# Seven products for two more pairs in the third group of both feed-forward stages, and another order at the head of the kernel

## The chip, the cores and the metric

The kernel runs on one core of one Trainium2 chip. The metric is the device time of one execution in microseconds (us); the time of a kernel is the median of its runs. Matmuls run on TensorE (PE, with its weight loads shown as PEld), elementwise work on VectorE (DVE) and ScalarE (ACT), and transfers are issued by SyncE (SP), by ACT's queue and by GpSimd (POOL).

## The reference

One layer of a hybrid encoder block over 256 tokens of width 2048, all in float32. The change concerns the two feed-forward stages (FFN 1 at the start, FFN 2 at the end) and the norm in front of FFN 1:

```python
x = x + 0.5 * swiglu(rms_norm(x, ffn1_norm[l]), ffn1_w_up[l], ffn1_w_down[l])
h = rms_norm(x, mix_norm[l])
proj = h @ w_in[l]
...                                   # two recurrent branches, gates, cross attention
x = x + 0.5 * swiglu(rms_norm(x, ffn2_norm[l]), ffn2_w_up[l], ffn2_w_down[l])
return rms_norm(x, final_norm)
```

with `swiglu(h) = (silu(gate) * up) @ w_down`, where `gate` and `up` are the halves of `h @ w_up`. The inner width is 5632.

## The kernel before, in words

**Precision.** Each float32 operand is split into a high part, rounded to the type `float32r` that PE multiplies, and a low part, the rest. A product is then three matmuls: high by high, low by high, high by low (`three`, L446). The high part is rounded by ACT (`split`, L120), the low part is the difference, taken by DVE (L121).

**Feed-forward order.** The 5632 inner columns fall into 11 groups (g = 0 to 10) of 512. For each group there are 8 *pairs* (p = 0 to 7), each 256 of the 2048 rows of the up weights, held in one weight tile of 128 x 2048 elements. Behind a group come *downs*: one tile of the down weights each, for an earlier group, 24 matmuls. Group 0 is followed by none, groups 1 and 2 by two downs each, groups 3 to 10 by four. `ffn_order` (L42) writes this order out, once for both stages; `PRODUCTS` (L458) says what each kind of pair multiplies:

- *plain* (group 0): 8 products, 24 matmuls.
- *fast*: a pair of 2 x 2 blocks by Strassen-like sums, 7 products, 21 matmuls. Its weights need sums of the blocks (`td`, three DVE subtractions, L213 to L215), and high and low parts of both the blocks and the sums: on ACT one rounding of 128 x 1536 and two of 128 x 1024, on DVE one difference of 128 x 1536 (`l`) and two of 128 x 1024 (`tl`).
- *mixed*: 8 products whose results fit the accumulators of a fast group; 24 matmuls, weights split as a plain tile.

Groups 1 and 2 alternate mixed and fast (four of each). From group 3 on p = 0 and p = 6 are mixed and the other six fast, in the order p = 1, 3, 0, 4, 2, 6, 5, 7.

**How a weight tile is prepared.** `weights` (L165) works through the plan of all tiles two ahead of their use. `prepare` (L195) has SP load the tile into one of three `raw` buffers (L71, taken in turn) and splits it into `h` and `l` (three buffers each). From group 3 on a mixed tile is *added* (L133): `begin_added` (L186), called one tile earlier, loads `raw`, has ACT write its rounded negative into `l` (L191) and has POOL issue a transfer that adds `raw` to that (`accum_op`, L192), which leaves the low part in `l`; `prepare` then only rounds `raw` into `h` (L200). No DVE work is in it, and 32 such transfers are in the kernel.

**Behind a group.** The eight accumulators are combined by DVE and ACT (`ends`, L529 to L532, when the last pair that uses accumulator 0 is through; `last`, L533 to L543), put through `activate` (L478), turned by PE transposes and split again (`turn`, L483, `hidop`).

**The head.** 16 matmuls on a tile of ones (`warm`, L109) run before the first data are there. ACT's queue loads the norm weights and small parameters (`vt`, 168 columns, L99). `head_x(p)` (L572) has SP load 512 columns of x for a pair, then `operand_pairs` (L406) scales them by the norm's weights on ACT into `xg` (two instructions of 128 x 256, L412) and splits `xg` into `xh` and `xl`. The first four weight tiles come in four cuts each. `rest` (L162) holds work put behind a given tile of the plan, such as the sums of x's blocks (L432) that fast and mixed pairs need. The first eight tiles are issued in program order on SP, ACT and DVE (L170, L179); after that the order is the scheduler's. `parameters` (L611), a chain of small ACT and DVE steps on `vt` for the recurrent branches, is called from `to_mix` (L642) and held behind the last residual update so far by `issue_after`.

Of the kernel before, what the change touches and what calls it, by code (L numbers as in the profile page):

```python
# [8 lines left out]
F32 = mybir.dt.float32  # L9
F32R = mybir.dt.float32r  # L10
ACT = mybir.ActivationFunctionType
ALU = mybir.AluOpType

P = 128
T = 256
# [12 lines left out]
VEC = {}  # L28
# [13 lines left out]
def ffn_order():  # L42

    out, down = [("plain", 0, p) for p in range(8)], [("down", 0, 1, c, 0) for c in range(4)]
    for g in range(1, NG):
        if g < 3:  # L50
            out += [(("mixed", "fast")[p % 2], g, p) for p in (0, 1, 2, 3, 5, 4, 7, 6)]
        else:
            out += [("mixed" if p in (0, 6) else "fast", g, p) for p in (1, 3, 0, 4, 2, 6, 5, 7)]
        if g > 2 and g % 2:
            down = [("down", g - 2, 2, c, b) for c in range(4) for b in (g - 2, g - 1)]
        n = 2 if g < 3 else 4
        out, down = out + down[:n], down[n:]
    return out + [("down", NG - 2, 2, c, b) for c in range(4) for b in (NG - 2, NG - 1)]
# [3 lines left out]
def block_kernel(ctx: ExitStack, tc: tile.TileContext, xT, xin, memT, vec, gfin, bgate, lruw, wu1, wd1, win, wv,  # L62
                 wg, wab, wout, wq, wk, wvm, wo, wu2, wd2, out_):
    nc = tc.nc
    pe, dve, act, sp = nc.tensor, nc.vector, nc.scalar, nc.sync
# [21 lines left out]
    def slot(dt=F32, name="slot"):  # L87
        return slots.tile([P, 1024], dt, name=name, tag="slot")
# [4 lines left out]
    def bank(name="acc"):  # L93
        return psum.tile([P, 512], F32, name=name, tag="acc")


    vt = const.tile([P, NVEC], F32, name="vt")
    small_n = VEC["ident"][0]
    act.dma_start(vt[:, :small_n], vec[:, :small_n])  # L99

    def col(name, i=0, n=1):
        a = VEC[name][0] + i
        return vt[:, a:a + n]
# [1 line left out]
    ones = const.tile([P, P], F32, name="ones")  # L105
    dve.memset(ones, 1.0)
    warm = bank("warm")
    for _ in range(16):
        pe.matmul(warm[:, :P], ones, ones, start=True, stop=True)  # L109
    eps = const.tile([P, 1], F32, name="eps")  # L110
    act.activation(eps, ones[:, :1], ACT.Copy, scale=EPS)
# [4 lines left out]
    done = {}  # L116


    def split(h, l, raw):
        done["high"] = act.activation(h, raw, ACT.Copy).ins  # L120
        done["low"] = dve.tensor_tensor(out=l, in0=raw, in1=h.bitcast(F32), op=ALU.subtract).ins  # L121
# [4 lines left out]

    plan, ahead = [], []
    orders = dict.fromkeys(("ffn1", "ffn2"), ffn_order())

    def plan_ffn(name, wu, wd):  # L130
        for e in orders[name]:
            src = wd[e[4], e[3]] if e[0] == "down" else wu[e[1], e[2]]
            kind = "fast" if e[0] == "fast" else "added" if e[0] == "mixed" and e[1] > 2 else "plain"  # L133
            plan.append(((name,) + e, src, kind))

    def plan_columns(name, w, which):
# [2 lines left out]
    def plan_rows(name, w, g):  # L139
        plan.extend(((name, g, kq), w[g, kq], "plain") for kq in range(w.shape[1]))  # L140

    plan_ffn("ffn1", wu1, wd1)
    for hf in range(2):
        for base in (8, 0):
# [11 lines left out]
    for name, w in (("mv", wvm), ("o", wo)):  # L156
        for g in range(4):
            plan_rows(name, w, g)
    plan_ffn("ffn2", wu2, wd2)

    head, rest = [], {}
# [204 lines left out]
    def root_ready(x):  # L366

        root = small.tile([P, 1], F32, name="root", tag="root")
        act.activation(root, x[:, :1], ACT.Abs)
        act.activation(root, root, ACT.Sqrt)  # L370
# [21 lines left out]
    def normed(ops, c, gain):  # L392

        accs = turned(xt[c])
        for m in range(4):
            ops.add(accs[m // 2][:, m % 2 * T:][:, :T], col(gain, 4 * c + m))
# [6 lines left out]
    BOTH = [2, 4]  # L403
    xd = []

    def operand_pairs(src, gain, q, xg, out):  # L406

        for a in src:
            i = len(out)
            g = xg[:, i * 512:(i + 1) * 512]  # L410
            for z in range(2):
                act.activation(g[:, z * T:][:, :T], a[:, z * T:(z + 1) * T], ACT.Copy,  # L412
                               scale=col(gain, 4 * q + 2 * i + z))
            h, l = slot(F32R, "xh"), slot(F32R, "xl")
            split(h[:, :512], l[:, :512], g)
            less = None if i else (h[:, 512:768], l[:, 512:768])
            if 2 * q + i in BOTH:
                if 2 * q + i == BOTH[0]:
                    xd.append(slot(F32R, "xd"))
                n = 512 * BOTH.index(2 * q + i)  # L420
                less = [xd[-1][:, a:a + 256] for a in (n, n + 256)]
            out.append(((h, l), less))

        def sums(which=((0, "less"), (0, "sums"), (1, "less"), (1, "sums"))):
            s = slot(name="xs")
            for i, ((h, l), less) in enumerate(out):
                a = [xg[:, i * 512 + j * P:][:, :P] for j in range(4)]

                def made(h, l, n, at, terms):
                    o = [s[:, at + j * P:][:, :P] for j in range(n)]  # L430
                    for j, (x, y, op) in enumerate(terms(o)):
                        dve.tensor_tensor(out=o[j], in0=x, in1=y, op=op)  # L432
                    split(h, l, s[:, at:at + n * P])

                if less and (i, "less") in which:
                    made(*less, 2, 0, lambda o: ((a[0], a[1], ALU.subtract), (a[2], a[3], ALU.subtract)))
                if (i or 2 * q in BOTH) and (i, "sums") in which:
                    if not i and len(which) > 1:
                        s = slot(name="xs")
                    made(h[:, 512:], l[:, 512:], 4, 512 * i,  # L440
                         lambda o: ((a[1], a[3], ALU.add), (o[0], a[0], ALU.subtract),
                                    (a[1], a[0], ALU.subtract), (a[2], o[1], ALU.subtract)))

        return sums
# [127 lines left out]
    def head_x(p):  # L572

        q = p // 2
        if p % 2 == 0:
            xq[q] = slot(name="xf"), slot(name="xg"), []
        src, xg, out = xq[q]
        a = p % 2 * 512
        sp.dma_start(src[:, a:a + 512], xT[:, p * 512:(p + 1) * 512])
        sums = operand_pairs([src[:, a:a + 512]], "ffn1_norm", q, xg, out)  # L580
        if p % 2:
            sums1.append(sums)
        pairs1.append(out[-1])

    def head_residual(i):
# [4 lines left out]
        if i:  # L590
            sp.dma_start(vt[:, small_n:NVEC], vec[:, small_n:])

    head += [lambda p=p: head_x(p) for p in range(8)]
    for i in range(2):
        rest[4 + i] = lambda i=i: head_residual(i)
# [46 lines left out]
    def to_mix(c, t):  # L642
        sq2.add(c, [t])
        if t == 0:
            return
        if c == 0:
            with tc.issue_after(done["residual"]):
                parameters()
        if c == 2:
            root_ready(xt[c])  # L650
        if c < 3:
            normed(xs2, c, "mix_norm")
        else:
            late2.append(lambda: normed(xs2, c, "mix_norm"))

    with scope(**FFN_POOLS):
        ffn("ffn1", pairs1, sq1, to_mix)
# [393 lines left out]
    def to_ffn(c):  # L1051
        out = []
        sums2.append(operand_pairs(turned(xt[c]), "ffn2_norm", c, slot(name="xg"), out))
        pairs2.extend(out)
        if c < 2:
            sums2.pop(0)()
# [130 lines left out]
```

## Time and profile before

| | |
|---|---|
| median of 3 runs | 2441.59 us (2441.09 to 2441.65) |
| the profiled execution's own time | 2441.09 us |
| its span | 2439.3 us |
| granted TensorE clock | 0.999 |
| PE busy | 2428.9 us (100% of the span), 12250 matmuls |
| DVE busy | 1889.8 us (77%) |
| ACT busy | 1394.5 us (57%) |
| DMA | 509.69 MB, 209 GB/s on average |
| accumulating transfers by POOL | 32 |

The profile shows one execution. The span is the stretch from the first to the last record; the execution's own time has 1.8 us more around it. A row of the timeline gives start, duration, engine, line, operation and `out<-in` tiles with their shape; `xN` is the number of like instructions put in one row, and brackets give the engine's idle time before the row with what ended it. A row of a table of stretches gives the stretch, its length, then busy time and number of instructions of PE, PE's weight loads, DVE, ACT and POOL, then clock, DMA share and GB/s. A row of waits names the waiting instruction, what it waited for, total us, times and longest. Matmuls are pipelined: one of 128 x 512 is shown with some 0.39 us, and the next starts before it ends.

### The profile page before, as it was taken

The numbers are of one execution on the slowest core, as the hardware profiler recorded it, in microseconds if no ns is written. First come the engines' busy times: TensorE is split into PE (matmuls) and PEld (weight loads), VectorE is DVE, ScalarE is ACT, GpSimd is POOL, SyncE is SP. The second block draws the span as 40 slices with busy tenths as digits, with TensorE's granted clock in tenths as the row PEclk, the third lists the DMA queues.
The fourth block names the chain that finished last, engine by engine and source line by source line (L and its number), as shares of the span: only waits on it lengthen the run. The fifth ranks groups of instructions, "written<-read, shape, count | busy, mean of one in ns | idle before, by whom it ended". The sixth has DMA issues, their size and how long they took to land.

```text
span 2439.3 us, 30196 instructions
## 1 busy us (share of the span) xinstructions
PE 2428.9 (100%) x12250; PEld 2034.0 (83%) x12250; DVE 1889.8 (77%) x2015; ACT 1394.5 (57%) x1399; POOL 28.1 (1%) x36
## 2 busy tenths in 40 slices
PE   9999999999999999999999999999999999999998
PEld 8888888888888888888888888888888888888887
DVE  7999999999865767577565676556589999999995
ACT  8566666666554454477435554455555666666664
POOL 0000000000000000000000000000000000000000
PEclk9999999999999999999999999999999999999999
DMA  7577767777655445445555555444555777777774
GB/s 293 194 224 258 250 233 236 234 238 237 214 188 190 173 173 182 173 172 216 194 186 190 209 192 188 172 172 156 190 190 187 249 238 233 234 238 242 237 234 150
DMA packets 75308, 509.69 MB, mean 209 GB/s; under 512 B 8352, under 2 KB 8608, under 8 KB 15264
## 3 DMA queue, kind: packets, MB, share of 16 engines
q1 hardware_dynamic: 69840, 473.06, 53.9%
q0 software_dynamic: 4608, 33.56, 6.8%
q8 instruction: 96, 1.57, 0.3%
q10 hardware_dynamic: 720, 1.13, 0.1%
q14 instruction: 44, 0.36, 0.0%
HBM read 472.07 MB, written 2.10 MB: 194 GB/s over the span
## 4 chain that ended last, share of the span: by engine, by line
PE 98%; DVE 1%; DMA 0%; ACT 0%; issue 0%; ACTq 0%; SPq 0%; DVEq 0%
PE acc L449 18%; PE acc L450 18%; PE acc L452 18%; PE acc L231 11%; PE acc L252 8%; PE acc L253 8%; PE acc L255 8%; PE acc L235 6%; PE acc L488 1%; PE acc L389 1%; DMA raw<-wu 0%; PE acc L764 0%; PE acc L1046 0%; PE acc L1001 0%; PE acc L867 0%; PE warm L109 0%
## 5 line engine op out<-in xcount | busy, mean ns | idle before, releaser
L121 DVE TENSOR_TENSOR l<-raw,h 128x2048 fp32r<-128x2048 f32 (+2 forms) x420 | 872.8, 2085 | 357.9 <-ACT h L120 346.1
L120 ACT ACTIVATE h<-raw 128x2048 fp32r<-128x2048 f32 (+2 forms) x420 | 732.8, 1752 | 626.2 <-PE acc L253 204.5
L449 PE MATMUL acc<-h,xh 128*128 128x512 f32 x1280 | 498.3, 390 | 0.4 <-ACT h L120 0.4
L450 PE MATMUL acc<-h,xl 128*128 128x512 f32 x1280 | 496.9, 389 | 0.0
L120 ACT ACTIVATE h<-td 128x1024 fp32r<-128x1024 f32 x224 | 229.2, 1055 | 180.1 <-PE acc L450 137.5
L252 PE MATMUL acc<-h,ops 128*128 128x512 f32 x832 | 326.9, 393 | 0.0
L253 PE MATMUL acc<-h,ops 128*128 128x512 f32 x832 | 324.3, 390 | 0.0
L121 DVE TENSOR_TENSOR tl<-td,h 128x1024 fp32r<-128x1024 f32 x224 | 267.0, 1220 | 32.3 <-ACT h L120 29.9
L449 PEld LDWEIGHTS acc<-h,xh 128*128 128x128 f32 x1280 | 240.3, 188 | 51.1 <-ACT h L120 1.1
L450 PEld LDWEIGHTS acc<-h,xl 128*128 128x128 f32 x1280 | 240.3, 188 | 49.5
L231 PE MATMUL acc<-ops,h 128*128 128x512 f32 x1152 | 278.0, 393 | 0.3
L449 PE MATMUL acc<-h,hidop 128*128 128x512 f32 x704 | 275.8, 392 | 0.0
L450 PE MATMUL acc<-h,hidop 128*128 128x512 f32 x704 | 274.3, 390 | 0.0
L231 PEld LDWEIGHTS acc<-ops,h 128*128 128x128 f32 x1152 | 211.9, 188 | 42.9 <-DVE ops L292 0.9
L452 PE MATMUL acc<-l,xh 128*128 128x512 f32 x832 | 218.6, 389 | 0.0
L255 PE MATMUL acc<-l,ops 128*128 128x512 f32 x832 | 206.1, 390 | 0.0
L452 PE MATMUL acc<-l,hidop 128*128 128x512 f32 x704 | 188.3, 389 | 0.0
L255 PEld LDWEIGHTS acc<-l,ops 128*128 128x128 f32 x832 | 156.2, 188 | 32.4
L252 PEld LDWEIGHTS acc<-h,ops 128*128 128x128 f32 x832 | 156.2, 188 | 32.3
L452 PEld LDWEIGHTS acc<-l,xh 128*128 128x128 f32 x832 | 156.1, 188 | 32.4
L253 PEld LDWEIGHTS acc<-h,ops 128*128 128x128 f32 x832 | 156.3, 188 | 31.6
L452 PEld LDWEIGHTS acc<-l,hidop 128*128 128x128 f32 x704 | 132.1, 188 | 27.5
(218 smaller groups left out, 2355.0 us busy)
## 6 DMA issues: line engine op xcount, KB each, us to landing
raw<-wu SPq DMA_DIRECT2D x172, 1024.0 KB, 4.9
raw<-wd SPq DMA_DIRECT2D x88, 1024.0 KB, 4.8
raw<-win SPq DMA_DIRECT2D x40, 1024.0 KB, 4.8
l<-raw POOLq DMA_DIRECT2D x32, 1024.0 KB, 7.3
raw<-wg SPq DMA_DIRECT2D x32, 1024.0 KB, 4.8
raw<-wab SPq DMA_DIRECT2D x16, 1024.0 KB, 4.8
raw<-wout SPq DMA_DIRECT2D x16, 1024.0 KB, 4.8
raw<-wq SPq DMA_DIRECT2D x16, 1024.0 KB, 4.8
```

The costliest lines, as they stand in the source:

```text
L120: done["high"] = act.activation(h, raw, ACT.Copy).ins
L121: done["low"] = dve.tensor_tensor(out=l, in0=raw, in1=h.bitcast(F32), op=ALU.subtract).ins
L231: pe.matmul(acc, h[:, k * P:(k + 1) * P], xs[k], start=k == 0, stop=False)
L235: done["product"] = pe.matmul(acc[:, :T], l[:, k * P:(k + 1) * P], xs[k][:, :T], start=False, stop=k == KT - 1).ins
L252: pe.matmul(accs[t], x[:, t * P:][:, :P], h[j], start=first and j == 0, stop=False)
L253: pe.matmul(accs[t], x[:, T + t * P:][:, :P], h[j], start=False, stop=False)
L255: done["product"] = pe.matmul(accs[t], x[:, t * P:][:, :P], l[j], start=False, stop=last and j == 3).ins
L389: pe.transpose(accs[m // 2][:, m % 2 * T + t * P:][:, :P], tile[:, t * 512 + m * P:][:, :P], ident)
L449: pe.matmul(acc, ah, bh, start=start, stop=False)
L450: pe.matmul(acc, al, bh, start=False, stop=False)
L452: pe.matmul(acc, ah, bl, start=False, stop=stop)
L488: pe.transpose(acc[:, z * T + t * P:][:, :P], hid[t][:, (2 * y + z) * P:][:, :P], ident)
```

## The change

1. In `ffn_order`, group 2 gets the order of the groups from 3 on: six fast pairs and two mixed ones for four and four; and in `plan_ffn` its two mixed tiles are of the kind *added*.
2. The load of `vt` is cut in two on ACT's queue: the 16 columns of the first norm's weights, then the other 152.
3. 13 warm matmuls for 16.
4. The first pair of x is no longer scaled into `xg` first: ACT rounds its first half and DVE its second half straight from the loaded `xf` into `xh`, and DVE makes both halves of `xl` from `xf`. Its `xg`, which the later sums read, is made behind the second weight tile (`rest[1]`).
5. `parameters` is also held behind the last rounding by ACT issued so far (`done["high"]`).

```diff
@@ ffn_order
-        if g < 3:
+        if g < 2:
             out += [(("mixed", "fast")[p % 2], g, p) for p in (0, 1, 2, 3, 5, 4, 7, 6)]
         else:
             out += [("mixed" if p in (0, 6) else "fast", g, p) for p in (1, 3, 0, 4, 2, 6, 5, 7)]
@@ block_kernel
-    act.dma_start(vt[:, :small_n], vec[:, :small_n])
+    first_n = VEC["mix_norm"][0]
+    for a, b in ((0, first_n), (first_n, small_n)):
+        act.dma_start(vt[:, a:b], vec[:, a:b])
...
-    for _ in range(16):
+    for _ in range(13):
         pe.matmul(warm[:, :P], ones, ones, start=True, stop=True)
@@ plan_ffn
-            kind = "fast" if e[0] == "fast" else "added" if e[0] == "mixed" and e[1] > 2 else "plain"
+            kind = "fast" if e[0] == "fast" else "added" if e[0] == "mixed" and e[1] > 1 else "plain"
@@ operand_pairs(src, gain, q, xg, out, later=None)
-            for z in range(2):
-                act.activation(g[:, z * T:][:, :T], a[:, z * T:(z + 1) * T], ACT.Copy,
-                               scale=col(gain, 4 * q + 2 * i + z))
             h, l = slot(F32R, "xh"), slot(F32R, "xl")
-            split(h[:, :512], l[:, :512], g)
+            by = [col(gain, 4 * q + 2 * i + z) for z in range(2)]
+
+            def scaled(g=g, a=a, by=by):
+                for z in range(2):
+                    act.activation(g[:, z * T:][:, :T], a[:, z * T:(z + 1) * T], ACT.Copy, scale=by[z])
+
+            if later is None:
+                scaled()
+                split(h[:, :512], l[:, :512], g)
+            else:
+                act.activation(h[:, :T], a[:, :T], ACT.Copy, scale=by[0])
+                dve.tensor_scalar(out=h[:, T:512], in0=a[:, T:], scalar1=by[1], scalar2=None, op0=ALU.mult)
+                for z in range(2):
+                    dve.scalar_tensor_tensor(out=l[:, z * T:(z + 1) * T], in0=a[:, z * T:(z + 1) * T], scalar=by[z],
+                                             in1=h[:, z * T:(z + 1) * T].bitcast(F32), op0=ALU.mult, op1=ALU.subtract)
+                later.append(scaled)
@@ head_x
-        sums = operand_pairs([src[:, a:a + 512]], "ffn1_norm", q, xg, out)
+        later = [] if p == 0 else None
+        sums = operand_pairs([src[:, a:a + 512]], "ffn1_norm", q, xg, out, later)
+        if later:
+            rest[1] = later[0]
@@ to_mix
-            with tc.issue_after(done["residual"]):
+            with tc.issue_after(done["residual"]), tc.issue_after(done["high"]):
                 parameters()
```

2 lines of the change are left out of this document (1 added, 1 removed).

## The prediction

> **What bounds the kernel now.** I began with the page's busy times, then asked what TensorE waited for, and then how full VectorE (DVE) is in the stretches that the change touches.
>
> ```profile
> span 2439.3 us, 30196 instructions
> PE 2428.9 (100%) x12250; PEld 2034.0 (83%) x12250; DVE 1889.8 (77%) x2015; ACT 1394.5 (57%) x1399; POOL 28.1 (1%) x36
> l<-raw POOLq DMA_DIRECT2D x32, 1024.0 KB, 7.3
> PE warm L109 <- DVE ones L106: 1.1, 1, 1.1
> PE acc L449 <- ACT h L120: 0.4, 1, 0.4
> ```
>
> PE is busy for all but 10.4 us of the span, and its only waits are 1.1 us at the start and 0.4 us late in FFN 2. So this kernel is its sequence of matmuls: a matmul that goes is a gain only while PE's supply keeps up. DVE, which makes the low parts of the weights, has 77% on average, but the third group is not an average place:
>
> ```profile
> 110.00:162.00 52.00, 52.00 (x232) 42.84 (x232) 50.66 (x50) 29.46 (x26) 1.00 (x1) 1.00 0.63 213
> 162.00:214.00 52.00, 52.00 (x234) 42.43 (x233) 48.90 (x48) 34.23 (x29) 0.86 (x1) 1.00 0.76 248
> 1836.00:1888.00 52.00, 52.00 (x234) 42.94 (x234) 48.15 (x48) 29.74 (x26) 0.86 (x1) 1.00 0.54 187
> ```
>
> Behind the length of the stretch stand the busy times, each with its count of instructions: PE, PE's weight loads, DVE, ACT, POOL. DVE is busy for 50.66 of 52 us in FFN 1's third group (g = 2) and the start of its fourth, 48.90 behind that, 48.15 in the third group of FFN 2. DVE has 1.34 us to spare in the first, 3.10 in the second, 3.85 in the third. PE does not wait there, but it has little behind it.
>
> **The change part by part.** The sum is made against the profiled execution: 2441.09 us, of which 2439.3 are span and 1.8 lie around it. The median of the runs is 2441.59, 0.5 above it.
>
> *Matmuls saved.* A mixed pair has 8 products of 3 matmuls, a fast one 7. In each FFN two pairs of group 2 turn from mixed to fast: 6 matmuls less, 12 in all. Two downs (48 matmuls) lie between these rows:
>
> ```profile
> 145.12 0.39 PE L449 MATMUL acc<-h,hidop 128*128 128x512 f32 x1
> ...
> 156.00 0.39 PE L449 MATMUL acc<-h,xh 128*128 128x512 f32 x1
> ```
>
> 10.88 / 48 = 0.227 us a matmul, so 12 × 0.227 = **2.72 us off PE's path**, 1.36 in each FFN, if nothing stalls.
>
> *DVE in group 2.* Before: four mixed pairs, split as plain, and four of the kind fast. After: six of the kind fast and two "added", whose low part ACT and a POOL accumulate make without DVE. The prices stand in one stretch of the DVE timeline, read from start to start:
>
> ```profile
> 101.61 2.28 DVE L121 TENSOR_TENSOR l<-raw,h 128x2048 fp32r<-128x2048 f32 x1
> ...
> 105.61 1.21 DVE L213 TENSOR_TENSOR td<-raw 128x1024 f32<-128x1024 f32 x1
> 106.75 1.75 DVE L121 TENSOR_TENSOR l<-raw,h 128x1536 fp32r<-128x1536 f32 x1
> 108.42 0.68 DVE L214 TENSOR_TENSOR td<-raw,td 128x512 f32<-128x512 f32 x1
> 109.02 1.22 DVE L121 TENSOR_TENSOR tl<-td,h 128x1024 fp32r<-128x1024 f32 x1
> 110.15 0.68 DVE L215 TENSOR_TENSOR td<-raw,td 128x512 f32<-128x512 f32 x1
> 110.75 1.28 DVE L493 TENSOR_TENSOR hidop<-acc,hidop 128x512 fp32r<-128x512 f32 x2
> 111.95 2.28 DVE L121 TENSOR_TENSOR l<-raw,h 128x2048 fp32r<-128x2048 f32 x1
> 114.15 1.22 DVE L121 TENSOR_TENSOR tl<-td,h 128x1024 fp32r<-128x1024 f32 x1
> ```
>
> A fast pair is L213 1.14 + l 1.67 + L214 0.60 + L215 0.60 + two tl of 1.13 = 6.27 us; a plain low part is 2.20. Two fast more and four plain less: 2 × 6.27 − 4 × 2.20 = +3.74 us of DVE per FFN, while PE's time for the group shrinks by 1.36. In FFN 1, 1.34 us are to spare: 3.74 + 1.36 − 1.34 = 3.8 us are missing, and PE, which comes 1.36 earlier, would wait for them: +2.4 us net by DVE's load alone. In FFN 2, 3.74 + 1.36 − 3.85 = 1.25 us are missing.
>
> *The chain through the raw buffers.* There are three raw buffers, used in turn. In the order of groups from 3 on, the raw loads are begun in the order p = 1, 0, 3, 4, 6, 2, 5, 7, an added pair one place early, so the loads of p = 0, p = 6 and p = 7 share one buffer. Each added pair holds it until ACT has negated it, POOL's accumulate has read it and ACT has rounded it. In FFN 1 the trace first has this chain in group 3:
>
> ```profile
> 153.88 1.00 POOL L192 DMA_DIRECT2D l<-raw  x1 [153.44 <-DVE l L121]
> 186.99 1.23 DVE L213 TENSOR_TENSOR td<-raw 128x1024 f32<-128x1024 f32 x1 [2.48 <-DMA raw<-wu]
> 192.14 2.44 DVE L121 TENSOR_TENSOR tl<-td,h 128x1024 fp32r<-128x1024 f32 x2
> 196.72 0.39 PE L449 MATMUL acc<-h,hidop 128*128 128x512 f32 x1
> ```
>
> From POOL's issue for p = 0 to the group's last tl it takes 194.58 − 153.88 = 40.7 us, and the group ends on PE 2.1 us later, at 196.72. DVE idles 2.48 us for the last raw, so transfers set this end, not DVE. Group 3 runs from 156.00 to 196.72 = 40.7 us without a stall only because its accumulate was issued 2.1 us ahead of the group's start. Its transfers are not the quick ones of the page; the stretch 150 to 200 has
>
> ```profile
> raw<-wu SPq DMA_DIRECT2D x6, 1024.0 KB, 5.3
> l<-raw POOLq DMA_DIRECT2D x2, 1024.0 KB, 11.7
> ```
>
> 11.7 us against 7.3 overall, beside the raw loads. The Trainium skill, page "DMA: Bandwidth & Descriptors", section "SWDGE vs HWDGE vs iDMA", says that the transfers of all issuing engines run on the same 16 DMA engines, which go round between the queues; by that rule four more accumulates in FFN stretches that are full of loads take their time from one another, and the row agrees; had the rule not held, the rival with quick accumulates below would be the forecast.
>
> Group 2 gets this chain. When does it start? In the changed order of ACT the negation for p = 0 stands behind the h of the first fast pair's td, which waits for DVE's L213; that stands where the plain l of 101.61 stood. So: L213 from 101.61, ready 102.75; ACT's h of 1.06 us until 103.8; a negation of 1.9 (the time of a 2048-wide ACT pass, see 37.11 below) until 105.7; POOL at about 106.0. Then the chain: 106.0 + 40.7 + 2.1 = 148.8 for the end of the group on PE, where before had 145.12: **+3.7 us**, the 1.36 saved already inside. From below: if the accumulates take the 7.3 us of the page, two are 8.8 us shorter and DVE's load sets the end (+2.4); below that only a lead that the windows do not show gives −1.36. From above: 13 us each, a little over 11.7, gives +6. I take 3.5, between the two mechanisms and near the chain.
>
> *Group 3 of FFN 1* follows after two downs only (10.9 us). All of group 2's final additions now come behind its last fast pair instead of partly beside its last mixed one, and DVE and ACT arrive late. The negation for its p = 0 then waits until PE has read the last of those downs (its ACT queue has the first fast h in front, and that h takes the buffer the down gives up): two ACT passes of 1.9 us behind the group's start, POOL 4 us behind it instead of 2.1 ahead. The chain then makes the group 4 + 40.7 + 2.1 = 46.8 us instead of 40.7: +6.1 at most; with the two accumulates at 7.3, or with the lead regained in the downs, 0 to 0.3. I take **+3.5**, the middle, since the row at 186.99 shows transfers as the limit but no row shows the start shifted. From group 4 on four downs (21.8 us) stand between groups, and the lead comes back.
>
> *FFN 2.* The one stall of the trace is here, 0.4 us, in group 3:
>
> ```profile
> 1885.51 0.86 POOL L192 DMA_DIRECT2D l<-raw  x1 [1280.06 <-ACT l L191]
> 1888.32 0.39 PE L449 MATMUL acc<-h,xh 128*128 128x512 f32 x1
> ```
>
> Its accumulate is issued 2.8 us ahead of the group, as in FFN 1. Group 2 enters FFN 2 with the supply prepared ahead, so the 1.25 us that are missing in DVE are likely covered: −1.36 (to +1). Group 3 loses some of its lead: +0.9 (−0.4 to +1.9). Sum **−0.5**.
>
> *The head.* Rows of the start:
>
> ```profile
> 1.05 6.23 PE L109 MATMUL warm<-ones 128*128 128x128 f32 x32 [1.05 <-DVE ones L106]
> 1.18 1.84 SPq L207 DMA_DIRECT2D raw<-wu  x4
> 4.44 0.21 ACT L623 ACTIVATE par<-vt 128x8 f32<-128x8 f32 x1 [1.77 <-DMA vt<-vec]
> 4.80 0.89 ACT L412 ACTIVATE xg<-xf,vt 128x256 f32<-128x256 f32 x2
> 6.25 2.48 ACT L120 ACTIVATE h<-raw 128x512 fp32r<-128x512 f32 x4
> 7.04 0.48 PE L449 MATMUL acc<-h,xh 128*128 128x512 f32 x1
> 8.74 0.91 ACT L412 ACTIVATE xg<-xf,vt 128x256 f32<-128x256 f32 x2
> 37.11 1.90 ACT L120 ACTIVATE h<-raw 128x2048 fp32r<-128x2048 f32 x1
> 39.81 0.39 PE L449 MATMUL acc<-h,xh 128*128 128x512 f32 x1
> 4.00:6.00 2.00, 2.00 (x11) 2.00 (x11) 0.00 (x0) 1.50 (x5) 0.00 (x0) 1.00 0.88 324
> 6.00:7.00 1.00, 1.00 (x10) 1.00 (x10) 0.62 (x2) 1.00 (x3) 0.00 (x0) 1.00 1.11 391
> ```
>
> The first real matmul (7.04) follows the warm passes at once; its h is ready 6.25 + 0.62 = 6.87. Three warm matmuls less are six passes: at the mean of 6.23 / 32 they would be 1.2 us. But the last two rows (passes in brackets) show 11 passes in 2 us up to 6.00 and 10 in the one us behind it: the late ones take 0.1, and if their speeding-up is set by time, six fewer save 0.1 × 6 = 0.6 to 0.7. ACT delivers the first h about 1 us earlier, since the two parameter steps at 4.44, one of the two xg and half of xh go. The later quarters of the first weight tile come when they land (four issues from 1.18 on), so I take 0.7 at the first matmuls (bounds 0.3 and 1.2). The Trainium skill, page "TensorE: Matmul & The Clock Gate", section "Part 1: The HAM clock gate", has PE at half clock until about 3.4 us of sustained work; an estimate by it, early passes twice as long as late, makes the six 0.8 us. The rows have the change of pace later, at some 5 us of work.
>
> That gain does not live. The deferred scaling puts two xg of 0.4 us each, 0.8 us, onto ACT ahead of the third pair, and from 8.74 on ACT and DVE take turns with only short idle time: h of the seventh pair is ready at 37.11 + 1.90 = 39.01, PE reads it at 39.81. With ACT 0.8 later and PE 0.7 earlier, 39.81 meets 39.11, and PE waits the 0.7 there. Net **0** (−0.7 if ACT's idle time hides the scaling, +0.3 if DVE, late by 0.8, touches group 1). The narrow transfer of the first norm weights gains nothing that reaches PE behind this, the 152 other columns are read later, and the parameter steps (two ACT passes of 0.2, small DVE ones) move from the head to the last downs of FFN 1: 0, at most +0.5.
>
> *Sum:* 3.5 + 3.5 − 0.5 + 0 = +6.5, so 2441.09 + 6.5 = 2447.6, and 2448 beside the median.
>
> **The rivals.**
> 1. *PE keeps its gain.* If PE's supply enters group 2 of FFN 1 with a lead of 4 us or more in its buffers (the 3.8 us that are missing there) and accumulates take near 7.3 us, nothing stalls: −2.72, the 0.4 stall gone perhaps, the head 0 to −0.7: **2438**, faster but by less than 0.2%. For it: not one wait of PE in FFN 1. Against it: DVE at 50.66 of 52. Chance 0.20.
> 2. *Only DVE's load counts.* +2.4 in group 2 of FFN 1, nothing in group 3, −0.5 in FFN 2: 2441.6 + 1.9 = **2443.5**, within 0.2%. For it: the wait of 2.48 us was hidden before. Chance 0.20.
> 3. *The transfers collide worse.* Accumulates of 13 us in both groups: +6, +6 and +1 in FFN 2: **2454**. For it: 11.7 in the one stretch like it, with only two accumulates in 50 us where there will be four. Chance 0.12.
> 4. *The change does not do what it says*: matmuls go, but the head gain is taken back by the deferred scaling. This is already in my sum; if the head kept it, each number is 0.7 lower.
>
> **How the numbers follow.** About 0.2% (4.9 us) is what a measurement of this kernel can tell from no change: 2436.7 to 2446.5 is "same". The forecast itself (2446.5 to 2452) has 0.45; a milder form of it, 2444 to 2446.5, goes with rival 2. Faster by over 0.2% would need all of 2.72 + 0.7 + 0.4 and another 1.1 us: 0.03. Same: 0.20 + 0.20 = 0.40. Slower: 0.45 + 0.12 = 0.57. The range from 2438 to 2455 takes in rivals 2 and 3 and the edge of rival 1.
>
> **What would show it.** Step by step: the trace has 12 matmuls fewer; PE waits for DVE or ACT appear between 103 and 149, and group 2 ends near 148.8, not 143.8; POOL's first issue near 106 and accumulates of 10 us and more in that stretch; the wait of DVE for raw before the last fast pair of groups 2 and 3; group 3 longer than 41 us; PE's first real matmul near 6.4 and level with before again at 40; FFN 2 shorter by about a microsecond or level. If PE shows no waits in 103 to 210, the lead was larger than DVE's idle time tells and rival 1 is right; if waits there end with DVE and never with a raw transfer, rival 2 is.

## The result, and the profile after

The changed kernel takes 2448.64 us (median of 8 runs, 2446.67 to 2449.30), the kernel before, beside it, 2441.31 (8 runs, 2440.80 to 2441.74). The ratio is 1.0029, 95% interval 1.0018 to 1.0040: slower by 4 to 10 us. The forecast was 2448. The profiled execution took 2446.67, 5.58 more than that of before; the traces explain these 5.6 us. The runs without a profile lie some 2 us higher still, which those of before do not; that part stays open (end of the section on the prediction).

The page of the changed kernel begins:

```profile
span 2444.9 us, 30205 instructions
PE 2430.3 (99%) x12232; PEld 2029.3 (83%) x12232; DVE 1898.3 (78%) x2033; ACT 1406.7 (58%) x1411; POOL 31.6 (1%) x40
```

PE's waits (total us, times, longest):

```profile
PE acc L464 <- ACT h L122: 2.1, 5, 0.5
PE acc L503 <- DVE hidop L508: 1.8, 3, 0.8
PE warm L111 <- DVE ones L108: 1.1, 1, 1.1
PE acc L467 <- DVE l L123: 0.3, 1, 0.3
```

And the stretches that the prediction started from (after the length: PE, weight loads, DVE, ACT, POOL):

```profile
110.00:162.00 52.00, 50.04 (x217) 39.13 (x216) 48.78 (x51) 32.89 (x28) 0.86 (x1) 1.00 0.71 235
162.00:214.00 52.00, 51.24 (x227) 41.07 (x226) 50.40 (x50) 35.25 (x29) 1.75 (x2) 1.00 0.80 263
1836.00:1888.00 52.00, 51.58 (x231) 42.08 (x230) 48.56 (x49) 34.24 (x29) 1.76 (x2) 1.00 0.75 243
```

PE has 18 records fewer: 12 matmuls and the six warm passes. It now waits for ACT's and DVE's output: once at 39.59, and otherwise in the groups that were changed and the ones next to them. DVE's busy time rose by 8.5 us (1898.3 − 1889.8).

Where did the time go? PE's own timeline gives the boundaries: the first row is the first real matmul, then the start of group 2, of the downs behind it, of group 3 and of its downs.

```profile
6.14 0.47 PE L464 MATMUL acc<-h,xh 128*128 128x512 f32 x1
...
39.59 0.50 PE L464 MATMUL acc<-h,xh 128*128 128x512 f32 x1 [0.39 <-ACT h L122]
...
103.86 0.39 PE L464 MATMUL acc<-h,xh 128*128 128x512 f32 x1
...
149.49 0.39 PE L464 MATMUL acc<-h,hidop 128*128 128x512 f32 x1
...
160.37 0.39 PE L464 MATMUL acc<-h,xh 128*128 128x512 f32 x1
...
202.60 0.39 PE L464 MATMUL acc<-h,hidop 128*128 128x512 f32 x1
```

| place | before | after | later than before |
|---|---|---|---|
| first real matmul | 7.04 | 6.14 | −0.90 |
| seventh pair of group 0 | 39.81 | 39.59 | −0.22; the matmul behind it −0.11 |
| start of group 2, FFN 1 | 103.28 | 103.86 | +0.58 |
| its downs | 145.12 | 149.49 | +4.37 |
| start of group 3 | 156.00 | 160.37 | +4.37 |
| its downs | 196.72 | 202.60 | +5.88 |
| start of group 2, FFN 2 | 1835.60 | 1841.39 | +5.79 |
| end of group 3, FFN 2 | 1929.56 | 1935.24 | +5.68 |

The start of group 2 before is this row:

```profile
103.28 0.39 PE L449 MATMUL acc<-h,xh 128*128 128x512 f32 x1
```

So the head gives 0.9 and loses 1.5 by the end of group 1; group 2 of FFN 1 costs 3.79; group 3 behind it 1.51; FFN 2 gives back a tenth.

The chain of waits of the stretch 100 to 150 is the one that the prediction drew, with somewhat other durations (start, us, what):

```profile
104.47 1.91 ACT l L193
...
106.70 11.51 DMA l<-raw
...
118.28 4.65 DMA raw<-wu
...
122.95 1.93 ACT l L193
...
125.18 8.84 DMA l<-raw
...
134.07 4.84 DMA raw<-wu
...
139.01 1.23 DVE td L215
...
148.73 0.76 DVE l L123
```

Negation, accumulate, load into the buffer set free, negation, accumulate, load, and DVE's work on the last fast pair: forecast with a start at 106.0 and the group's end at 148.8, found with 106.70 and 149.49. But the chain is not the whole of it. PE does not wait at its end; it waits early and in the middle. From the timelines of PE, ACT and DVE:

```profile
113.81 0.33 PE L503 MATMUL acc<-vt,ev 128*128 128x128 f32 x1 [0.77 <-DVE hidop L508]
122.95 1.92 ACT L193 ACTIVATE l<-raw 128x2048 fp32r<-128x2048 f32 x1 [2.75 <-DMA raw<-wu]
124.77 1.04 ACT L122 ACTIVATE h<-td 128x1024 fp32r<-128x1024 f32 x1
125.84 1.23 DVE L123 TENSOR_TENSOR tl<-td,h 128x1024 fp32r<-128x1024 f32 x1 [2.79 <-ACT h L122]
```

and the first 13 us of the group as a stretch, in the changed kernel and before:

```profile
103.00:116.00 13.00, 11.34 (x49) 7.70 (x47) 13.00 (x15) 8.54 (x7) 1.00 (x1) 1.00 0.76 195
103.00:116.00 13.00, 13.00 (x62) 10.64 (x62) 13.00 (x14) 6.28 (x6) 0.00 (x0) 1.00 0.59 201
```

In the first 13 us of the group DVE is busy for 13.00 of 13 while PE already stands still at times (113.81 is one of several places). DVE was as full there before, and PE did not wait: a full supplier shows that there is nothing to spare, not yet that it is late. What changed is what PE gets for DVE's time. By the prediction's prices a fast pair takes 6.27 us of DVE for 21 × 0.227 = 4.8 us of PE, a mixed pair split as plain 2.20 for 5.4. The old order alternates them; the new one begins with two fast pairs. Then, at 122.95, ACT's queue stands behind the second negation, which waits 2.75 us for its load; the `h` behind it comes late, and DVE, already short of time, idles 2.79 us for that `h`. That is two causes, and the experiments had to part them.

Group 3 loses its 1.51 us elsewhere. From start to start of its matmuls, all but 0.2 us of the loss lies before 171.4. The chain of the stretch 158 to 204 runs there through DVE, with one break of any length, 0.45 us, and reaches PE from it:

```profile
157.57 1.20 DVE x L573 x2
...
169.21 1.22 DVE tl L123
170.48 0.73 PE acc L467 x2
```

The first of these rows is still the work behind the downs. No transfer stands in this chain.

### The profile page after: what moved, and what is told of

Its sections match the earlier page's. It is cut to its first block, busy times and chain, and to the rows that moved or that the text cites. A ratio compares the mean times of both kernels' runs of the same rounds, so it can differ in the third digit from the quotient of the medians.

```text
span 2444.9 us, 30205 instructions
## 1 busy us (share of the span) xinstructions
PE 2430.3 (99%) x12232; PEld 2029.3 (83%) x12232; DVE 1898.3 (78%) x2033; ACT 1406.7 (58%) x1411; POOL 31.6 (1%) x40
## 4 chain that ended last, share of the span: by engine, by line
PE 91%; DVE 4%; DMA 3%; ACT 1%; issue 1%; ACTq 0%; SPq 0%; DVEq 0%
PE acc L467 16%; PE acc L464 16%; PE acc L465 16%; PE acc L233 11%; PE acc L254 8%; PE acc L255 8%; PE acc L257 8%; PE acc L237 6%; DMA raw<-wu 1%; DMA l<-raw 1%; DVE l L123 1%; PE acc L503 1%; DVE tl L123 1%; PE acc L391 1%; ACT h L122 1%
## 5 line engine op out<-in xcount | busy, mean ns | idle before, releaser
L123 DVE TENSOR_TENSOR l<-raw,h 128x2048 fp32r<-128x2048 f32 (+2 forms) x416 | 862.6, 2079 | 355.8 <-ACT h L122 344.0
L122 ACT ACTIVATE h<-raw 128x2048 fp32r<-128x2048 f32 (+2 forms) x416 | 723.8, 1746 | 612.4 <-PE acc L255 205.8
L122 ACT ACTIVATE h<-td 128x1024 fp32r<-128x1024 f32 x232 | 237.7, 1055 | 172.1 <-PE acc L465 134.2
L123 DVE TENSOR_TENSOR tl<-td,h 128x1024 fp32r<-128x1024 f32 x232 | 277.2, 1221 | 35.5 <-ACT h L122 33.0
```

## The experiments

Each kernel ran in five rounds beside the kernel before.

**The new group 2 alone** (g2_only: on the kernel before, the head untouched).

```diff
-        if g < 3:
+        if g < 2:
...
-... else "added" if e[0] == "mixed" and e[1] > 2 else "plain"
+... else "added" if e[0] == "mixed" and e[1] > 1 else "plain"
```

> The kernel before with the new group 2 alone (its order and its two added pairs, both FFNs), the head as before. Both theories: first real matmul at 7.04, PE level with before until group 2 of FFN 1 starts (103.28). DVE theory (DVE is short of time as soon as fast pairs follow one another behind the downs): most of the stall of FFN 1's group 2 lies in its first 13 us, ahead of any effect of the raw buffers, some 3 us, and the whole kernel is 4 to 5 us slower than before, 2445.5 to 2446.5. Chain theory (accumulate, raw buffer, accumulate, raw buffer sets the end): the same sum, but the stall lies in the second half of the group, ending with a raw transfer. Rival (the head's loss of 0.58 us is what tipped group 2): no stall of over 1 us, about 2440.

Measured: 2447.50 us, ratio 1.0027 (1.0017 to 1.0038). Group 2 starts at 103.27, level with before, and its downs at 148.80: 45.53 us long for 41.84, +3.69. Group 3 takes 42.63 for 40.72. So group 2 does by itself nearly all of the change's loss; the rival by which the head tips it is out. The total is 1.0 us above the highest that was expected. The stalls of PE in group 2 add up to 5.05 us (3.69 and the 1.36 that six matmuls fewer should give); from start to start of its matmuls, beyond 0.227 us each and the 1.03 us that the group's eight transposes take before, some 3.2 of them lie before 116, where DVE is busy throughout, and the other 1.8 from 124.5 on. Each theory had named one of these places.

**The same order without accumulates** (g2_plain).

```diff
-        if g < 3:
+        if g < 2:
             out += [(("mixed", "fast")...
```

> The kernel before with the new order of group 2, but its two mixed pairs split as plain ones (DVE makes their low part, POOL does nothing): 12 matmuls fewer, DVE +8.1 us in each FFN's group 2 (2 x 6.27 - 2 x 2.20), no accumulates in it. Chain theory: without accumulates no chain, so group 2 of FFN 1 is less slow than with added pairs, +0 to +2.5, total below 2444. DVE theory: 8.1 + 1.36 - 1.34 = 8.2 us missing in FFN 1's group 2, so it ends about 6.8 us later than before (152), group 3 loses more on top, and the kernel takes 2448 to 2453.

Measured: 2451.56 us, 1.0042 (1.0029 to 1.0054). No accumulate runs in group 2, and it is worse: the chain theory alone falls, DVE's load alone makes a loss of this size. The total is in the range of the DVE theory, the places are not: group 3 starts 1.8 us late (157.76), not 6.8; the end of group 3 is 6.3 late, and FFN 2, of which the expectation did not speak, loses another 3.9. 1.6 us of the 6.3 are not DVE's time but a slower PE behind a wait (last section). DVE in the profile of this kernel, in the group and at the start of the next:

```profile
103.00:145.00 42.00, 40.32 (x177) 31.62 (x176) 42.00 (x41) 25.24 (x22) 0.00 (x0) 1.00 0.50 184
156.00:168.00 12.00, 10.21 (x40) 7.92 (x39) 12.00 (x14) 5.61 (x5) 1.00 (x1) 0.86 0.68 175
```

Busy for 42.00 of 42 us and for 12.00 of 12. (The clock in the second row, 0.86, belongs to that slower PE.)

**The other way round: more accumulates, less DVE** (old_added: order and matmuls of before, but the four mixed pairs of group 2 are added; DVE has 8.8 us less per FFN).

```diff
-... else "added" if e[0] == "mixed" and e[1] > 2 else "plain"
+... else "added" if e[0] == "mixed" and e[1] > 1 else "plain"
```

> The order and matmuls of before, but the four mixed pairs of group 2 are of the kind added: DVE is relieved of 4 x 2.20 = 8.8 us in each FFN's group 2, and four accumulates more run there in each. DVE theory: nothing stalls, the total is that of before, 2440.8 to 2441.5. Chain theory: four accumulates in turn through three raw buffers, each with some 10 us, make FFN 1's group 2 several us longer, total over 2443.

Measured: 2454.68 us, 1.0053 (1.0039 to 1.0067). Here the DVE theory fails as a theory of everything: with 8.8 us of DVE work less, and all matmuls of before, FFN 1's group 2 takes from 103.23 to 150.60, 47.4 us for 41.84. PE's largest wait, and what stands ahead of it, from the timelines:

```profile
116.80 0.77 PE L449 MATMUL acc<-h,xh 128*128 128x512 f32 x1 [3.90 <-DVE hidop L493]
113.69 1.23 DVE L213 TENSOR_TENSOR td<-raw 128x1024 f32<-128x1024 f32 x1 [2.42 <-DMA raw<-wu]
100.22 0.86 POOL L192 DMA_DIRECT2D l<-raw  x1 [7.97 <-DVE xs L432]
```

DVE idles 2.42 us for a raw load, and the `hidop` that PE wants stands behind it. The chain ahead of 117 has that load from 99.99 to 113.60: 13.61 us for one tile, beside the accumulate issued at 100.22, which took 14.3; the median load of this stretch (100 to 205) takes 6.2. So here the transfers' time reaches PE, through DVE's queue.

**Four raw buffers** (g2_raw4: the new group 2 alone; two slots given up for the room).

```diff
-    rawp = pool("raw", 3)
+    rawp = pool("raw", 4)
-    slots = pool("slots", 24)
+    slots = pool("slots", 22)
```

> The new group 2 alone, with four raw buffers for three (and 22 slots for 24, to make room). The loads of the two added pairs and of the last fast pair no longer share one buffer. In the run with three buffers FFN 1's group 2 stalled 2.9 us in its first 13 us, with DVE busy throughout, and 1.7 us from 125 on, behind a negation on ACT that waited for its raw load. DVE theory: the early stall stays, only the late one goes: group 2 ends 2 us later than before for 3.7, group 3 gains a little, total 2443.5 to 2445.5. Chain theory (my prediction's step): the whole delay of groups 2 and 3 goes, total 2439 to 2440.5.

Measured: 2444.00 us, 1.0012 (1.0003 to 1.0021), in the range of the DVE theory; 3.5 us less than with three buffers. Group 2 takes 103.26 to 146.50, 43.24 us: of the 3.69 us of g2_only 2.3 are gone and 1.4 stay. ACT's second negation no longer waits (the row that answers to 122.95 above), and the early stall is there as in g2_only:

```profile
118.91 1.91 ACT L191 ACTIVATE l<-raw 128x2048 fp32r<-128x2048 f32 x1
```

and the stretches up to 116 and from there to the group's end:

```profile
103.00:116.00 13.00, 11.26 (x50) 8.19 (x49) 13.00 (x14) 9.04 (x9) 1.00 (x1) 1.00 0.63 163
116.00:146.50 30.50, 30.50 (x135) 25.08 (x134) 29.03 (x28) 22.88 (x19) 0.86 (x1) 1.00 0.85 280
```

PE is idle for 1.74 us up to 116 and not at all behind that. The accumulates are not quicker in this run (10.0 us in the median between 100 and 150; 11.51 and 8.84 in the chain above), so it is the shared buffer, not the transfer, that was taken away.

**The control** (before_raw4: the kernel before with the same two pool sizes).

> The kernel before with four raw buffers (and 22 slots): a control. Both theories: PE waits only 0.4 us late in FFN 2 in the run with three, so the time is that of before within 0.6 us, 2440.6 to 2441.5; if it is faster or slower by more, part of what four buffers brought to the new group 2 has nothing to do with group 2.

Measured: 2441.14 us, 0.9999 (0.9990 to 1.0008). Four buffers bring nothing to the kernel before; what they bring is group 2's.

**The added pair in front** (on the new group 2 alone: g2_mixed_first, three buffers; raw4_mixed_first, four).

```diff
-            out += [(...) for p in (1, 3, 0, 4, 2, 6, 5, 7)]
+            out += [(...) for p in ((0, 1, 3, 4, 2, 6, 5, 7) if g == 2 else (1, 3, 0, 4, 2, 6, 5, 7))]
```

> The new group 2 alone, with its first added pair in front (p = 0, 1, 3, 4, 2, 6, 5, 7 for 1, 3, 0, 4, 2, 6, 5, 7), so that the group begins with a pair for which DVE has nothing to do. The same matmuls, accumulates and DVE work. DVE theory, with the place of the cover as the point: the early stall of 2.9 us falls under 1 us, the group ends within 1.5 us of before, total 2440 to 2442.5. Theory of the mere sum of DVE's time (3.8 us are missing wherever they fall): the stall moves to later pairs, total 2445 to 2447. Chain theory: the accumulate starts earlier by a pair, some 4 us, so the end of the group comes 3 to 4 us earlier as well, 2442 to 2443.

> The new group 2 alone with four raw buffers, and its first added pair in front (p = 0, 1, 3, 4, 2, 6, 5, 7). With three buffers this order had no early stall, but one of 4.65 us at 134 behind a raw load, and PE at half its pace for some 3 us behind it. Theory (two separate causes: the start without cover costs 2.7 us, the shared raw buffer the rest): both are gone, FFN 1's group 2 takes under 41.5 us (41.8 before, 43.2 with four buffers alone), total 2438.5 to 2441. Rival (DVE's missing 3.8 us come out somewhere in groups 2 and 3 whatever the order): total 2443 to 2446. Rival (the accumulates' own time decides when the first pair stands in front): a stall at 103 to 110 behind ACT or POOL, over 2444.

Measured: 2451.44 us with three buffers (1.0042, 1.0029 to 1.0054) and 2444.03 with four (1.0011, 1.0002 to 1.0020). With three the early stall is gone, as the place-of-cover theory said, but the total lies 4 us above the highest of the three forecasts: ACT waits for a raw load, and PE for ACT.

```profile
131.93 1.48 ACT L120 ACTIVATE h<-raw 128x1536 fp32r<-128x1536 f32 x1 [5.13 <-DMA raw<-wu]
134.41 0.80 PE L449 MATMUL acc<-h,xh 128*128 128x512 f32 x1 [4.48 <-ACT h L120]
```

The stretches of that wait and behind it (the figure after POOL is the granted clock; the 14 matmuls from 134.41 on take 6.13 us for some 3.2, so about 2.9 of the 4 us are lost behind the wait):

```profile
125.00:134.40 9.40, 4.54 (x19) 3.10 (x18) 5.03 (x6) 4.22 (x3) 0.00 (x0) 0.96 0.88 266
134.40:140.60 6.20, 6.19 (x15) 4.85 (x16) 6.20 (x6) 1.06 (x1) 0.00 (x0) 0.51 0.60 209
```

With four buffers neither of the two big stalls is there, and group 2 with its downs takes 103.17 to 155.79, 52.62 us for before's 52.72. Group 2 itself takes 41.24, under the 41.5 of the theory. Yet the total falls to its rival and is that of the usual order with four buffers: group 3 now runs 155.79 to 198.87, 43.08 us for 40.72. In g2_raw4 it takes 42.23, so part of the shortage came out one group later, and 1.5 us stand in group 3 in either order. From the start of group 2 to the end of group 3 it is 95.70 us here, 96.36 in g2_raw4, 93.44 before: +2.3 and +2.9 (2.6 and 3.2 beside the control's 93.14), where the prediction's sum over DVE alone had +2.4.

**All four downs ahead of group 2** (g2_downs4: on the new group 2 alone, three buffers).

```diff
-        n = 2 if g < 3 else 4
+        n = (4, 0)[g - 1] if g < 3 else 4
```

> The new group 2 alone, with all four downs of group 0 behind group 1 and none behind group 2, so that DVE has 21.8 us of cover ahead of group 2 and none ahead of group 3. If group 2 falls short only for its lead: its own stall goes (it ends about 1 us earlier in its own length than before), and the stall of 4 us or more comes in group 3, total 2445 to 2449. If something within the group (chain, raw buffers) sets its length, group 2 stays as long as with two downs ahead, and the total is over 2449.

Measured: 2448.94 us, 1.0031 (1.0019 to 1.0044), at the upper end of the first expectation: moving the cover moves the stall, it does not remove it. Group 2 now stalls 1.7 us (at 127) for 5.05 in g2_only, and group 3, with no downs ahead of it, some 6 us (waits of PE between 157 and 164 and again at 188).

**FFN 2 alone** (raw4_ffn2: four buffers, and only FFN 2 has the new group 2; 6 matmuls fewer).

```diff
-def ffn_order():
+def ffn_order(n_old):
...
-        if g < 3:
+        if g < n_old:
...
-    orders = dict.fromkeys(("ffn1", "ffn2"), ffn_order())
+    first_added = {"ffn1": 3, "ffn2": 2}
+    orders = {name: ffn_order(n) for name, n in first_added.items()}
...
-... else "added" if e[0] == "mixed" and e[1] > 2 else "plain"
+... else "added" if e[0] == "mixed" and e[1] >= first_added[name] else "plain"
```

> Four raw buffers, and the new group 2 in FFN 2 alone (6 matmuls fewer). With the new group 2 in both FFNs and four buffers, FFN 2 up to group 3's end was 0.7 us shorter than before. Theory (FFN 2 has the lead that FFN 1 lacks): 2440.2 to 2440.9, below the control with four buffers by 0.5 to 1.4 us. Rival (the saving is taken back there as well): level with the control.

Measured: 2440.99 us, 0.9999 (0.9990 to 1.0008), against the control's 2441.14: the difference, 0.15, is less than the spread of either, so nothing that can be told from zero, and short of the 0.5 forecast. The traces show the rival: group 2 of FFN 2 takes 40.68 us for the control's 41.78, and group 3 takes it back, 41.69 for 40.70.

**The head alone** (head_only: all edits but those of group 2), and **the head with the deferred scaling on GpSimd** (head_pool).

```diff
 def scaled(g=g, a=a, by=by):
     for z in range(2):
-        act.activation(g[:, z * T:][:, :T], a[:, z * T:(z + 1) * T], ACT.Copy, scale=by[z])
+        o, i_ = g[:, z * T:][:, :T], a[:, z * T:(z + 1) * T]
+        if later is None:
+            act.activation(o, i_, ACT.Copy, scale=by[z])
+        else:
+            nc.gpsimd.tensor_scalar(out=o, in0=i_, scalar1=by[z], scalar2=None, op0=ALU.mult)
```

> The changed kernel with group 2 as before: the head's edits alone (first pair rounded from its load, vt in two transfers, 13 warm matmuls, parameters later). My prediction's step: first real matmul 0.9 us earlier, level with before again at about 40 us where ACT's two deferred scalings arrive, and 0 to +0.6 us at the end of group 1, so 2441.3 to 2441.9. Rival (the head's gain is kept): 2440.4. Rival (the lag grows in group 2, whose margins are small): over 2442.5.

> The head's edits alone, with the two deferred scalings of the first pair's xg made by GpSimd (POOL) and not by ACT. If ACT's 0.8 us is what takes the head's gain back, PE is still about 0.8 us ahead of before at 40 us and on to the end of group 1, and the kernel takes 2440.4 to 2440.7. If the supply of group 0 eats any gain of the head whoever scales, it is level with head_only, 2441.3 to 2441.9.

Measured: head_only 2442.09 us (1.0004, 0.9995 to 1.0013), head_pool 2441.14 (0.9999, 0.9990 to 1.0008). Neither total lies in a range that was forecast: head_only is 0.2 above its own, head_pool between its two. In head_only PE is 0.98 us ahead at its first real matmul and 0.58 behind at 92.4 us. In head_pool it is 0.74 ahead there, still 0.68 ahead at 40 us, and level at the downs of group 1:

```profile
6.30 0.48 PE L468 MATMUL acc<-h,xh 128*128 128x512 f32 x1
...
92.42 0.39 PE L468 MATMUL acc<-h,hidop 128*128 128x512 f32 x1
```

(before: 7.04 and 92.40.) So the deferred scaling on ACT costs the 0.6 to 1.0 us between the two kernels, and it is what ended the gain at 40 us. Without it the gain is lost all the same, 35 to 50 us later, at 75 and 88 us, where PE reads an `h` that ACT has just made. Both expectations for head_pool were half right: ahead at 40, and the gain gone in the end.

The lead at the first real matmul is a figure of one execution each. In the eleven profiles whose head is that of before (its own among them) that matmul starts anywhere from 6.78 to 7.55. What hardly varies is the time from there to the downs of group 1: 85.3 to 85.5 us in these kernels (but for raw4_mf_sums, below), 86.8 and 86.9 with the new head, 86.1 in head_pool. So the new head loses 1.4 us on the way, 0.7 to 0.8 of it by ACT's scaling.

**Less DVE work ahead of group 2** (raw4_mf_sums: raw4_mixed_first, with the sums of x's blocks on GpSimd).

```diff
-                    dve.tensor_tensor(out=o[j], in0=x, in1=y, op=op)
+                    nc.gpsimd.tensor_tensor(out=o[j], in0=x, in1=y, op=op)
```

> The new group 2 in both FFNs, four raw buffers, the added pair in front, and the sums of x's blocks (L432, 32 instructions of 128 x 128 on DVE up to group 2 of FFN 1, 0.2 us each from start to start, 6.4 us) made by GpSimd. In the run without this last edit DVE was busy for 57.91 of 58 us ahead of group 2 and 52.31 of 53 in it, PE stalled some 1.2 us in group 2 and 2.3 in group 3, and the time was 2444.03. Theory (what is left after the buffers is DVE's load): 6.4 us less ahead of group 2 cover the 3.8 that are missing there, as far as three h and l buffers let DVE run ahead; the stalls of groups 2 and 3 fall under 1.5 us together, total 2439 to 2441.5. Rival (the lead cannot be carried over the group's boundary, since the buffers for prepared weights are full): 2443 to 2444.5. Rival (GpSimd's sums take longer than DVE's and are waited for in groups 0 and 1): over 2444.5.

Measured: 2446.02 us, 1.0021 (1.0012 to 1.0031): slower than without the edit. Its stretches show why (45 to 103 is group 1 with its downs, 103 to 156 mostly group 2 and its downs):

```profile
45.00:103.00 58.00, 55.87 (x247) 45.22 (x247) 53.22 (x52) 39.50 (x36) 14.86 (x14) 1.00 0.58 191
103.00:156.00 53.00, 53.00 (x238) 43.74 (x237) 51.65 (x54) 32.43 (x28) 0.86 (x1) 1.00 0.69 238
```

From the timelines of POOL, ACT and PE of this kernel:

```profile
60.60 3.79 POOL L432 TENSOR_TENSOR xs<-xg 128x128 f32<-128x128 f32 x2
67.23 0.63 ACT L120 ACTIVATE xh<-xs 128x512 fp32r<-128x512 f32 x1 [6.04 <-POOL xs L432]
106.43 0.39 PE L449 MATMUL acc<-h,xh 128*128 128x512 f32 x1
146.97 0.39 PE L449 MATMUL acc<-h,hidop 128*128 128x512 f32 x1
```

In the group that DVE was relieved for, PE is busy for 53.00 of 53 us, and group 2 takes 40.54 us, 1.30 less than before: here the six matmuls fewer are a gain at last. It is paid for in group 1, where ACT waits 6.04 us for GpSimd's sums and PE is idle for 2.1 us. PE comes to group 2 3.15 us later for it, which gave DVE time as well, and the run does not part the two. Group 3 still takes 42.17 us. Theory and last rival both happened, in different groups, and the total is the rival's. None of these kernels beats the one before.

## Why the prediction was right, point by point

- **12 matmuls, 2.72 us.** Right as a count, and as a bound: raw4_mf_sums shows group 2 shorter by 1.30 when nothing stalls.
- **DVE short by 3.8 us in FFN 1's group 2, +2.4 net.** Right in size, over groups 2 and 3 together: with the raw buffers out of the way the loss there is 2.3 to 2.9 us in either order of pairs. Not right in place: the prediction had all of it in group 2, the runs have 1.5 us or more of it in group 3. That PE loses nothing in group 2 when DVE is relieved (raw4_mf_sums) speaks for it, though PE was also 3.15 us late there.
- **The chain through the raw buffers, +3.7, of which 3.5 taken.** Measured +3.79. The chain's times were right to 0.7 us, and a fourth buffer takes 2.3 us off. But the step said that its end on DVE sets the group's end, where PE would wait. It does not: DVE waits 0.39 us for the last load. The chain hurts 15 us earlier, where a negation in ACT's queue waits for its load and the `h` that DVE and PE need stands behind it. The prediction treated the two causes as alternatives, 3.7 by the chain or 2.4 by DVE; in the runs they add up, 1.4 us that a fourth buffer leaves and 2.3 that it takes away. That the sum is so near the term is luck.
- **Group 3 of FFN 1, +3.5.** Measured +1.51: the mis-sized term, and by another mechanism. POOL's first issue came 2.9 us behind the group's start, not 4, and the two accumulates there took 8.1 us in the median, not the 11.7 carried over from the old group 3. More than that: a late accumulate did not make the group late. The prediction had read the old group 3 as free of stalls only because its accumulate was issued 2.1 us ahead; here it is issued 2.9 behind, and PE loses 0.2 us from 171.4 to the group's end. What PE waits for is the first part of the reasoning, the work behind group 2 that makes DVE late (the chain up to 170.48).
- **FFN 2, −0.5.** Measured −0.1, at the edge of what a run tells; its group 2 gave 0.54 of the 1.36, its group 3 took 0.43 back. With four buffers (raw4_ffn2) it is 1.10 and 0.99, near the −1.36 and +0.9 of the sum.
- **The head, 0.** Measured +0.58, more than the +0.3 that was named as the upper bound. Right to 40 us, in mechanism and place: there PE waits for ACT's `h`, and the lead falls from 0.81 to 0.11, the 0.7 forecast. The rest is lost at 75 and 88 us, 0.24 and 0.42, both times at an `h` that ACT has just made. At 88 the path can be followed: DVE is some 0.7 us late at 70, a load of down weights is issued 0.66 late for it (78.62) and takes 6.4 us, and ACT waits 1.31 us for it. In head_only and head_pool that load takes 6.5 and 6.4 us too, and ACT waits 1.40 and 1.31 us; before, the loads there take 5.4 at most, and ACT waits for none. So DVE's lateness is part of it, as the bound had it, and a longer load the other. Why the load is longer under the new head was not shown.
- **The warm passes.** The first real matmul came at 6.14, not 6.4; it changed nothing later. The difference is less than what kernels with one and the same head show (last section).
- **The sum.** Forecast 3.5 + 3.5 − 0.5 + 0 = +6.5; measured 3.79 + 1.51 − 0.11 + 0.58 = +5.8, of which 0.1 to 0.2 come back in the later downs, and 5.58 is the difference of the two profiled executions. Group 3 was 2.0 too high, the other three terms together 1.3 too low. The nearness of 2448 to the median is therefore partly luck: terms that were off against one another, and 1.7 us of the median's +7.3 that are not in the profiled execution.

**What stays open.** The changed kernel's runs without a profile lie at 2447.85 to 2449.30, its profiled one at 2446.67; g2_only spreads from 2446.36 to 2450.85. With four raw buffers the spread is less (2443.59 to 2445.35, profiled 2444.05). That fits transfer times that vary and enter through the shared buffer, but no trace of a longer run is at hand, and it was not shown. Nor did any run have a fourth `h` buffer. A fast pair takes two of the three, and ACT waits for PE to give one up in these groups too (1.0 us at most in group 2, 3.5 in the downs behind it), so it is not known how far more of them would let DVE and ACT work ahead.

## What to carry to other kernels

Where one engine is busy 100% and its supplier is nearly full (here VectorE had 1.3 to 3.9 us to spare in 52), count the supplier's work for an edit before the matmuls it saves: here 2.72 us of TensorE were to be had for 7.5 us of VectorE. An instruction that waits for a transfer costs what stands behind it in its queue, not only what needs its result; look for it in the middle of a chain, not only at the end. And moving cover or order about without taking work off the short engine moved the stall, here mostly to the next group.

## What the runs showed of the hardware that was not expected

**A stall of PE can cost more than its length.** The rows of g2_mixed_first above show it: after a wait of 4.48 us PE had a granted clock of 0.51 from 134.4 to 140.6. In g2_plain the matmuls behind a wait of 1.79 us (gap by the records; 1.95 us beyond the usual pace) start 0.43 us apart for 0.227:

```profile
161.08 1.48 PE L452 MATMUL acc<-l,xh 128*128 128x512 f32 x3 [1.79 <-DVE l L121]
162.36 0.63 PE L449 MATMUL acc<-h,xh 128*128 128x512 f32 x1
162.79 0.63 PE L450 MATMUL acc<-h,xl 128*128 128x512 f32 x1
163.21 0.63 PE L449 MATMUL acc<-h,xh 128*128 128x512 f32 x1
```

until 164.5, some 3.4 us: 1.6 us lost on top. Other waits of nearly the same length (1.92 us at 71.8 in raw4_mf_sums) were followed by the usual pace. The Trainium skill, page "TensorE: Matmul & The Clock Gate", section "Part 1: The HAM clock gate", has PE fall to half clock after at least one idle window of about 3.4 us. The trace differs from it: less than 2 us of idleness were enough at 161. In the changed kernel's profile no wait behind the warm passes is over 0.8 us, and its stretches show a clock of 1.00.

**The time at which PE quickens at the start differs between executions.** In all 14 profiles the first warm pass starts at 1.04 to 1.06 us, and the passes go from 0.21 us apart to 0.11. That change comes 2.9 us behind the first pass in old_added, 5.1 before and 6.1 in before_raw4, with the same head in all three. Where it comes late, the passes hold up the first real matmul (7.55 in before_raw4). So what three warm matmuls fewer are worth can't be read from one execution of each kernel.

**GpSimd is no cheap place for small sums.** The same 128 x 128 operations by groups of lines, in raw4_mixed_first up to 160 us (DVE; busy us, mean ns)

```profile
L432 DVE TENSOR_TENSOR xs<-xg 128x128 f32<-128x128 f32 x20 | 5.2, 283 | 0.0
```

and in the whole of raw4_mf_sums (POOL):

```profile
L432 POOL TENSOR_TENSOR xs<-xg 128x128 f32<-128x128 f32 x40 | 34.6, 887 | 1156.3 <-ACT xg L412 1111.0 <-ACT h L120 26.5 <-DVE xl L121 17.2
```

0.28 us against 0.89 on average, and in the row at 60.60 above 1.9 each. The profile's spans on POOL are rough, but ACT's wait of 6.04 us for these sums, above, is not one of them.
